# Down projections with one 512-column and one 256-column matmul per weight block

## The chip, the cores and the metric

The kernel runs on one core of a Trainium2 chip. The metric is device time in microseconds: the median of three runs, 1199.04 us before (1196.93 to 1201.48).

## The reference, cut to what matters

One layer of a hybrid decoder trunk on a sequence of 256 tokens with a model width of 2048, in float32: adaLN, a combined input projection, attention heads beside Mamba-2 heads, an output projection, and then a gated MLP with a causal depthwise convolution of width 3 over 5632 hidden channels. The change concerns the MLP's last product:

```python
def conv_ffn(h, w_up, conv_w, conv_b, w_down):
    u = causal_dwconv(h @ w_up, conv_w, conv_b)
    g, val = jnp.split(u, 2, axis=-1)
    return (jax.nn.silu(g) * val) @ w_down
...
x = x + gate_f * conv_ffn(h, w_up[l], conv_ffn_w[l], conv_ffn_b[l], w_down[l])
return rms_norm(x, final_norm_g)
```

## The kernel before, in words

All activations lie transposed: channels on the 128 partitions, the 256 tokens along the free axis. A float32 product is made from three matmuls in the format fp32r: weights w and activations a are each split into a high part (the value cast to fp32r) and a low part (the value less its high part), and the kernel adds w_hi·a_hi + w_hi·a_lo + w_lo·a_hi. `mm3` (lines 276 to 279) issues these three for one block of 128x128 weights; each is 256 columns wide and has a weight load of its own in the trace. An activation tile has 512 columns, the high part in the first 256 and the low part in the next 256.

Weights come in units. For a down projection a unit is 11 blocks (128 x 1408). SyncE's queue loads it, ScalarE casts it to the high part (line 258), VectorE subtracts to get the low part (line 259), in two parts of 8 and 3 blocks. High and low parts have four buffers each, so two units are ready or in use at a time, and the cast of a part waits until the part four back has been read by TensorE.

The MLP's 44 hidden tiles are done in two halves of 22. In each half the up projections fill 22 tiles `gts` of gated activations, and then a loop over the 16 column blocks i of the output (lines 803 to 822) multiplies them by the down weights: two units of 11 blocks, q = 0 and 1, added into one accumulator of 256 columns in PSUM, which has three accumulator buffers (`acc_tile`). There are 2 x 16 x 22 = 704 such blocks.

In half 0 two column blocks share a bank: block i even uses columns 0 to 255, i odd columns 256 to 511, and after the odd one ScalarE copies all 512 to `d0` (line 814). In half 1 each column block has a bank of its own; VectorE adds gate times `d0` to the residual stream x, then gate times the accumulator (`resid_add`, line 753). ScalarE squares x for the last norm (line 589), VectorE sums the squares, and ScalarE multiplies x by the norm's gain. Behind the sixteenth, three matmuls by ones sum over the partitions (lines 604 to 606), ScalarE takes the root, VectorE the reciprocal, and four products scale x and send it out.

The framework's scheduler sets each engine's order of instructions by a simulated timeline; an engine then works through its own queue in that order, with semaphore waits between engines.

The other products use the same helpers with other shapes: the value projections (line 348) stream 352 or 336 columns of weights, and the state space stage has a few matmuls of 512 columns in the same format (lines 557 and 558).

Of the kernel before, what the change touches and what calls it, by code (L numbers as in the profile page):

```python
# [18 lines left out]
T = 256  # L19
# [75 lines left out]
def hymba_layer(ctx, tc, xT, c_row, cT, w_ada, vecs, consts, relb, onehot, w_vdt, w_in, w_out, w_up1, w_up, w_dn, outT):  # L95
    nc = tc.nc
    dve, act, pool, pe = nc.vector, nc.scalar, nc.gpsimd, nc.tensor
# [30 lines left out]
    def acc_tile(name):  # L128
        return psp.tile([P, 512], F32, tag="acc", name=name, bufs=NACC)
# [63 lines left out]
    def V(name, i, n=1):  # L193
        return vec[:, CV[name] + i:CV[name] + i + n]
# [45 lines left out]
    def ada_some(n, last=24):  # L240
        for _ in range(n):
            g, i = ada_next[0]
            if g < last:
                ada_unit(g, i)
                ada_next[0] = [g, i + 1] if i < 3 else [g + 1, 0]
# [19 lines left out]
    def weight_unit(src, n, name, hw=1024):  # L265
        ws = get_unit(src, n, name)
        parts = [hi_lo_part(ws, o, min(hw, n - o), name) for o in range(0, n, hw)]

        def block(i):
            wh, wl = parts[i * P // hw]  # L270
            j = i * P % hw
            return wh[:, j:j + P], wl[:, j:j + P]

        return parts, block

    def mm3(o, whs, wls, a, first, last):
        pe.matmul(o, whs, a[:, 0:T], start=first, stop=False)  # L277
        pe.matmul(o, whs, a[:, T:2 * T], start=False, stop=False)  # L278
        pe.matmul(o, wls, a[:, 0:T], start=False, stop=last)  # L279

    def gemm_pair(acc, unit, b0, acts, npair=2):
        blk = unit[1]
        n = len(acts)
        for w in range(npair):
            o = acc[:, w * T:(w + 1) * T]
            for i, a in enumerate(acts):
                mm3(o, *blk(b0 + w * n + i), a, i == 0, i == n - 1)

    def gemm_part(o, unit, acts, first, last):
        blk = unit[1]  # L290
        n = len(acts)
        for i, a in enumerate(acts):
            mm3(o, *blk(i), a, first and i == 0, last and i == n - 1)


    def rstd_of(ps, n, name):
# [6 lines left out]
    def sqrt_ready(dep):  # L303
        act.activation(scr, dep, AF.Sqrt, bias=eps_t, scale=0.0)
# [120 lines left out]
    st = {}  # L425
# [158 lines left out]
    def sq_acc(i, name):  # L584
        if i == 0:
            act.activation(sqx, x[:, i, :], AF.Square)
        else:
            sq = tmp(f"sq_{name}", tag="psq", bufs=2)
            act.activation(sq, x[:, i, :], AF.Square)
            if i < 14:  # L590
                dve.tensor_add(sqx, sqx, sq)
            else:
                late_sq.append(sq)
# [100 lines left out]
    for i in range(6):  # L694
        pe.matmul(ss1[:, 0:T], ones, (sqs[:, 1, i * T:i * T + T] if i < 4 else sqs[:, 0, (i - 4) * T:(i - 3) * T]),
                  start=i == 0, stop=i == 5)
# [45 lines left out]
    def gate_up(j, us):  # L742
        g, v = (conv_ff(us[s], s * 44 + j, f"{j}_{s}") for s in range(2))
        act.activation(g, g, AF.Silu)
        dve.tensor_mul(v, g, v)
        gt = gp.tile([P, 512], F32R, tag="g", name=f"g{j}")
        hilo(gt, v)
        return gt

    d0 = fp.tile([P, KT, T], F32, name="d0")  # L750

    def resid_add(i, o, gate):
        dve.scalar_tensor_tensor(x[:, i, :], o, gate, x[:, i, :], op0=ALU.mult, op1=ALU.add)
# [15 lines left out]
    for j in range(NHALF):  # L769
        if j < NLEAD:  # L770
            acc = lead[j]
        else:
            u = weight_unit(w_up1[j], 2048, f"u1_{j}")
            acc = acc_tile(f"u1a{j}")
# [7 lines left out]
    for half in range(2):  # L782
        gts = []
        for jj in range(NHALF):
            j = half * NHALF + jj
            if half == 0:
                w = weight_unit(w_up1[NHALF + j], 2048, f"u2_{j}")
                acc = acc_tile(f"u2a{j}")
                gemm_pair(acc, w, 0, hk[8:])
                dve.tensor_add(parts[j], parts[j], acc)  # L790
                us = [parts[j][:, s * T:(s + 1) * T] for s in range(2)]
            else:
                acc = acc_tile(f"ua{j}")
                us = [acc[:, s * T:(s + 1) * T] for s in range(2)]
                for s in range(2):
                    gemm_part(us[s], weight_unit(w_up[2 * jj + s], 2048, f"u{j}_{s}"), hk, True, True)
            gts.append(gate_up(j, us))
            if half == 1:
                ada_some(1)
        if half == 1:  # L800
            ada_some(100)
            dve.tensor_add(par[:, 80:96], mod[:, 80:96], V("b_ada", 80, 16))
        for i in range(KT):
            if half == 0 and i % 2:
                o = acc[:, T:2 * T]
            else:
                acc = acc_tile(f"da{half}_{i}")
                o = acc[:, 0:T]
            for q in range(2):
                w = weight_unit(w_dn[half, i, q], 11 * P, f"d{half}_{i}_{q}")  # L810
                gemm_part(o, w, gts[11 * q:11 * q + 11], q == 0, q == 1)
            if half == 0:
                if i % 2:
                    act.copy(d0[:, i - 1:i + 1, :].rearrange("p a t -> p (a t)"), acc)
            else:
                gate = par[:, 80 + i:81 + i]
                resid_add(i, d0[:, i, :], gate)
                resid_add(i, o, gate)
                sq_acc(i, f"d{i}")
                act.activation(x[:, i, :], x[:, i, :], AF.Copy, scale=V("g_fin", i))  # L820
                if i == 0:
                    sqrt_ready(sqx[:, 0:1])
# [3 lines left out]
    for a, b in ((0, 2), (2, 6), (6, 11), (11, 16)):  # L826
        o = x[:, a:b, :]
# [89 lines left out]
```

## Time and profile before

| | |
|---|---|
| median of three runs | 1199.04 us |
| the profiled execution, its own time | 1196.57 us |
| its span, first to last instruction | 1194.8 us |
| matmuls on TensorE, busy | 1167.5 us, 9760 records |
| VectorE busy, ScalarE busy | 915.0 us, 636.9 us |
| mean granted clock | 0.988 |

Busy time of TensorE counts overlapping records once, and the ends of its records are modelled; the pace of a stream of matmuls is read from their starts. The first half's down projections run from about 703 to 824 us, the second half's from about 1068 to 1181.5.

### The profile page before, as it was taken

How to read it: one execution, taken by the hardware profiler on the slowest of the kernel's cores; microseconds unless marked ns; L12 is line 12 of the kernel's file. 1: busy time of each engine (PE TensorE's matmuls, PEld its weight loads, DVE VectorE, ACT ScalarE, POOL GpSimd, SP SyncE). 2: the span in 40 equal slices, each digit the busy share in tenths (PEclk: the TensorE clock that was granted, in tenths of full speed). 3: DMA queues.
4: the chain of work that ended last, by engine and by line, in shares of the span. 5: the costliest groups of instructions: out<-in, count | busy, mean ns of one | idle time of the engine just before them, and what ended most of it. 6: DMA issues, size and time to landing. Idle time of an engine off the chain costs nothing.

```text
span 1194.8 us, 23406 instructions
## 1 busy us (share of the span) xinstructions
PE 1167.5 (98%) x9760; PEld 1113.3 (93%) x9760; DVE 915.0 (77%) x1371; ACT 636.9 (53%) x959; POOL 0.9 (0%) x7
## 2 busy tenths in 40 slices
PE   6999999999999999999999999999999999999996
PEld 3899989988878898999999999999999999999995
DVE  6889979987988798786599984446888889656554
ACT  4544434457786544446567654444555555555552
POOL 0000000000000000000000000000000000000000
PEclk8899999999999999999999999999999999999998
DMA  9989988776765996997565545558878776545552
GB/s 359 409 338 337 327 335 304 276 268 246 287 242 214 365 383 237 343 357 245 183 204 186 201 146 194 195 194 276 295 299 301 284 282 227 196 150 196 194 194 96
DMA packets 47444, 309.60 MB, mean 259 GB/s; under 512 B 5568, under 2 KB 6761, under 8 KB 16105
## 3 DMA queue, kind: packets, MB, share of 16 engines
q1 hardware_dynamic: 46170, 307.04, 70.6%
q8 instruction: 76, 1.25, 0.4%
q10 hardware_dynamic: 1168, 1.06, 0.4%
q14 instruction: 30, 0.25, 0.1%
HBM read 305.98 MB, written 2.11 MB: 258 GB/s over the span
## 4 chain that ended last, share of the span: by engine, by line
PE 96%; DVE 1%; DMA 1%; ACT 1%; SPq 0%; issue 0%; DVEq 0%; ACTq 0%
PE ua L278 7%; PE ua L279 7%; PE da L279 7%; PE da L278 7%; PE da L277 7%; PE ua L277 7%; PE wa L277 6%; PE wa L279 6%; PE wa L278 6%; PE va L348 4%; PE u1a L278 3%; PE u1a L279 3%; PE u1a L277 3%; PE u2a L277 3%; PE u2a L279 3%; PE u2a L278 3%
## 5 line engine op out<-in xcount | busy, mean ns | idle before, releaser
L258 ACT CAST h_u<-s_u 128x1024 fp32r<-128x1024 f32 x176 | 183.6, 1050 | 188.3 <-PE ua L278 95.2
L259 DVE TENSOR_TENSOR l_u<-s_u,h_u 128x1024 fp32r<-128x1024 f32 x176 | 213.4, 1223 | 66.6 <-ACT h_u L258 64.6
L277 PE MATMUL ua<-h,h_u 128*128 128x256 f32 x704 | 194.3, 276 | 0.0
L278 PE MATMUL ua<-h,h_u 128*128 128x256 f32 x704 | 194.3, 276 | 0.0
L279 PE MATMUL ua<-h,l_u 128*128 128x256 f32 x704 | 194.3, 276 | 0.0
L279 PE MATMUL da<-g,l_d 128*128 128x256 f32 x704 | 194.3, 276 | 0.0
L278 PE MATMUL da<-g,h_d 128*128 128x256 f32 x704 | 194.3, 276 | 0.0
L277 PE MATMUL da<-g,h_d 128*128 128x256 f32 x704 | 194.1, 276 | 0.0
L259 DVE TENSOR_TENSOR l_d<-s_d,h_d 128x1024 fp32r<-128x1024 f32 (+1 forms) x128 | 108.8, 888 | 83.6 <-ACT h_d L258 83.6
L277 PE MATMUL wa<-hT,h_w 128*128 128x256 f32 x576 | 162.1, 282 | 0.8 <-ACT h_w L258 0.8
L279 PE MATMUL wa<-hT,l_w 128*128 128x256 f32 x576 | 159.8, 279 | 0.0
L278 PE MATMUL wa<-hT,h_w 128*128 128x256 f32 x576 | 159.7, 278 | 0.0
L258 ACT CAST h_d<-s_d 128x1024 fp32r<-128x1024 f32 (+1 forms) x128 | 98.2, 782 | 115.0 <-PE da L278 104.3
L210 DVE SCALAR_TENSOR_TENSOR ada<-ada,cb 128x2048 f32<-128x2048 f32 x60 | 137.2, 2288 | 11.5 <-DMA ada<-w_ada 11.2
L279 PEld LDWEIGHTS da<-g,l_d 128*128 128x128 f32 x704 | 132.2, 188 | 0.0
L277 PEld LDWEIGHTS ua<-h,h_u 128*128 128x128 f32 x704 | 132.2, 188 | 0.0
L278 PEld LDWEIGHTS ua<-h,h_u 128*128 128x128 f32 x704 | 132.2, 188 | 0.0
L279 PEld LDWEIGHTS ua<-h,l_u 128*128 128x128 f32 x704 | 132.2, 188 | 0.0
L278 PEld LDWEIGHTS da<-g,h_d 128*128 128x128 f32 x704 | 132.2, 188 | 0.0
L277 PEld LDWEIGHTS da<-g,h_d 128*128 128x128 f32 x704 | 132.1, 188 | 0.0
L258 ACT CAST h_w<-s_w 128x1024 fp32r<-128x1024 f32 x72 | 73.7, 1048 | 88.3 <-PE wa L278 42.7
L277 PEld LDWEIGHTS wa<-hT,h_w 128*128 128x128 f32 x576 | 108.4, 188 | 11.3 <-ACT h_w L258 3.6
(236 smaller groups left out, 2689.4 us busy)
## 6 DMA issues: line engine op xcount, KB each, us to landing
ada<-w_ada SPq DMA_DIRECT2D x96, 1024.0 KB, 6.1
s_u<-w_up SPq DMA_DIRECT2D x88, 1024.0 KB, 5.0
s_d<-w_dn SPq DMA_DIRECT2D x64, 704.0 KB, 4.1
s_w<-w_in SPq DMA_DIRECT2D x36, 1024.0 KB, 7.1
s_o<-w_out SPq DMA_DIRECT2D x16, 1024.0 KB, 8.3
s_v<-w_vdt SPq DMA_DIRECT2D x8, 1040.0 KB, 6.6
x<-xT SPq DMA_DIRECT2D x4, 512.0 KB, 4.8
outT<-x SPq DMA_DIRECT2D x2, 640.0 KB, 3.0
```

Of the source, the lines that this page charges most:

```text
L210: dve.scalar_tensor_tensor(ws[:, :D], ws[:, :D], 1.0, cb, op0=ALU.mult, op1=ALU.mult, accum_out=mod[:, j:j + 1])
L258: act.copy(wh[:, :m], ws[:, o:o + m])
L259: dve.tensor_sub(wl[:, :m], ws[:, o:o + m], wh[:, :m].bitcast(F32))
L277: pe.matmul(o, whs, a[:, 0:T], start=first, stop=False)
L278: pe.matmul(o, whs, a[:, T:2 * T], start=False, stop=False)
L279: pe.matmul(o, wls, a[:, 0:T], start=False, stop=last)
L348: pe.matmul(va[tt][i][:, :n], lo if st == 2 else hi, (wl if st == 1 else wh)[:, s], start=f and st == 0, stop=l and st == 2)
```

## The change

A new helper `gemm_full` takes the place of `gemm_part` in the down projections. It multiplies the high part of a weight block by all 512 columns of an activation tile at once, into all 512 columns of the accumulator's bank, so that w_hi·a_hi stands in the first 256 columns and w_hi·a_lo in the other 256; the low part of the weights is multiplied by the first 256 columns as before. In the last block the order of the two is turned round. Each column block has a bank of its own in both halves, and the two halves of the bank are added when it is read out: in half 0 ScalarE copies the first and VectorE adds the second to `d0`; in half 1 VectorE adds both to x, with the gate.

```diff
+    def gemm_full(acc, unit, acts, first, last):
+        blk = unit[1]
+        n = len(acts)
+        for i, a in enumerate(acts):
+            whs, wls = blk(i)
+            st, sp = first and i == 0, last and i == n - 1
+            if sp:
+                pe.matmul(acc[:, 0:T], wls, a[:, 0:T], start=False, stop=False)
+                pe.matmul(acc, whs, a, start=st, stop=True)
+            else:
+                pe.matmul(acc, whs, a, start=st, stop=False)
+                pe.matmul(acc[:, 0:T], wls, a[:, 0:T], start=False, stop=False)
...
         for i in range(KT):
-            if half == 0 and i % 2:
-                o = acc[:, T:2 * T]
-            else:
-                acc = acc_tile(f"da{half}_{i}")
-                o = acc[:, 0:T]
+            acc = acc_tile(f"da{half}_{i}")
             for q in range(2):
                 w = weight_unit(w_dn[half, i, q], 11 * P, f"d{half}_{i}_{q}")
-                gemm_part(o, w, gts[11 * q:11 * q + 11], q == 0, q == 1)
+                gemm_full(acc, w, gts[11 * q:11 * q + 11], q == 0, q == 1)
             if half == 0:
-                if i % 2:
-                    act.copy(d0[:, i - 1:i + 1, :].rearrange("p a t -> p (a t)"), acc)
+                act.copy(d0[:, i, :], acc[:, 0:T])
+                dve.tensor_add(d0[:, i, :], d0[:, i, :], acc[:, T:2 * T])
             else:
                 gate = par[:, 80 + i:81 + i]
                 resid_add(i, d0[:, i, :], gate)
-                resid_add(i, o, gate)
+                resid_add(i, acc[:, T:2 * T], gate)
+                resid_add(i, acc[:, 0:T], gate)
```

## Rows read from the trace of the kernel before

**Rows 1.** The page: busy us and share by engine, slices, chain that ended last.

```profile
PE 1167.5 (98%) x9760; PEld 1113.3 (93%) x9760; DVE 915.0 (77%) x1371; ACT 636.9 (53%) x959; POOL 0.9 (0%) x7
...
PE   6999999999999999999999999999999999999996
PEld 3899989988878898999999999999999999999995
...
PE 96%; DVE 1%; DMA 1%; ACT 1%; SPq 0%; issue 0%; DVEq 0%; ACTq 0%
```

**Rows 2.** The tile da: duration ns min/median/max, first and last start us, forms.

```profile
L277 PE MATMUL da<-g,h_d x704: 276/276/276, 702.9 to 1181.3; 128*128 128x256 f32 x176
...
L279 PE MATMUL da<-g,l_d x704: 276/276/277, 703.2 to 1181.5; 128*128 128x256 f32 x176
L753 DVE SCALAR_TENSOR_TENSOR x<-da,par,x x16: 483/484/485, 1071.1 to 1181.9; 128x256 f32<-128x256 f32 x16
L814 ACT COPY d<-da x8: 580/581/582, 718.4 to 823.7; 128x512 f32<-128x512 f32 x8
```

**Rows 3.** Timeline of TensorE, 740 to 745 (start us, busy us); 47 rows.

```profile
739.76 0.28 PE L278 MATMUL da<-g,h_d 128*128 128x256 f32 x1
739.88 0.28 PE L279 MATMUL da<-g,l_d 128*128 128x256 f32 x1
...
744.98 0.28 PE L279 MATMUL da<-g,l_d 128*128 128x256 f32 x1
```

**Rows 4.** Windows: us, busy and count by engine, granted clock, DMA share, GB/s.

```profile
1086.00:1181.00 95.00, 95.00 (x841) 95.00 (x840) 50.07 (x74) 48.10 (x73) 0.00 (x0) 1.00 0.51 168
```

**Rows 5.** Timeline of TensorE, state space stage: 512 columns and what follows.

```profile
333.85 0.39 PE L558 MATMUL sg<-am,tri_r 128*128 128x512 f32 x1
334.08 0.28 PE L559 MATMUL sg<-am,ones_r 128*128 128x256 f32 x1
...
345.64 0.39 PE L558 MATMUL sg<-am,tri_r 128*128 128x512 f32 x1
345.86 0.28 PE L559 MATMUL sg<-am,ones_r 128*128 128x256 f32 x1
...
346.58 0.28 PE L277 MATMUL oa<-cat,h_o 128*128 128x256 f32 x1
...
374.50 0.40 PE L558 MATMUL sg<-am,tri_r 128*128 128x512 f32 x1
374.75 0.28 PE L559 MATMUL sg<-am,ones_r 128*128 128x256 f32 x1
```

**Rows 6.** Chain in order of time (start us, us): the value projections.

```profile
170.43 11.40 PE va L348 x72
```

**Rows 7.** Timeline of TensorE beside the value projections; nine rows.

```profile
228.33 0.28 PE L278 MATMUL wa<-hT,h_w 128*128 128x256 f32 x1
...
229.27 0.33 PE L348 MATMUL va<-l_v,hT 128*128 128x352 f32 x1
```

**Rows 8.** Lines by form, 900 to the end: busy us, mean ns, idle before.

```profile
L259 DVE TENSOR_TENSOR l_d<-s_d,h_d 128x1024 fp32r<-128x1024 f32 x32 | 39.1, 1221 | 23.0 <-ACT h_d L258 23.0
L258 ACT CAST h_d<-s_d 128x1024 fp32r<-128x1024 f32 x32 | 33.6, 1049 | 47.6 <-PE da L278 45.5 <-issue 1.2 <-PE ua L278 0.8
...
L737 ACT ACTIVATE fo<-ua,vec 128x256 f32<-128x256 f32 x32 | 17.9, 559 | 1.4 <-DVE fo L739 1.4
```

**Rows 9.** Waits, 1071 to 1181: us in total, times, longest us.

```profile
ACT h_d L258 <- PE da L278: 45.2, 28, 2.2
```

**Rows 10.** Timeline of ScalarE and VectorE, 1173.2 to 1176.

```profile
1173.24 1.53 ACT L258 CAST h_d<-s_d 128x1024 fp32r<-128x1024 f32 x2 [2.21 <-PE da L278]
...
1174.37 0.48 DVE L753 SCALAR_TENSOR_TENSOR x<-da,par,x 128x256 f32<-128x256 f32 x1 [2.10 <-PE da L279]
1174.77 1.69 DVE L259 TENSOR_TENSOR l_d<-s_d,h_d 128x1024 fp32r<-128x1024 f32 x2
```

**Rows 11.** Chain in order of time, from 1181 to the end.

```profile
1181.70 0.13 PE da L279
1181.83 0.03 issue
1181.86 0.49 DVE x L753
1182.35 0.02 issue
1182.37 0.42 ACT sq_d L589
1182.80 0.04 issue
1182.84 0.71 PE ssx L606 x2
```

## The prediction

> **What bounds the kernel now.** I read the page from the top: the engine totals, the slices and the chain of waits. The reader is to see in [rows 1] that TensorE's matmuls fill 98% of the span, that both middle rows of the slices hold nines from the third slice to the last but one, and that TensorE makes 96% of the chain that ended last. Next I read the down projections' tile: 2112 matmuls of 256 columns, 704 from each of three lines, all at one duration [rows 2]. Their ends are modelled, so I take the pace from their starts in the timeline: 47 rows from 739.76 to 744.98 are 46 steps in 5.22 us, or 113.5 ns a matmul [rows 3]. A long stretch of the second half's down projections shows TensorE and its weight loads busy for all of 95.00 us, at a granted clock of 1.00 [rows 4]. At the upper of the two clock levels, 2.4 GHz, 256 columns are 106.7 ns, so each matmul carries 6.8 ns beyond its columns. A block is three of them now: 340.4 ns. All 704 blocks make 239.6 us, and this is the only time that the change can move, apart from the end of the kernel.
>
> **The change part by part.**
>
> *The matmuls.* Each block loses one 256-column matmul and its weight load, and another becomes 512 columns wide. The columns stay at 768. So nothing of the 320 ns that the columns take at 2.4 GHz goes away; what can change is the 20.4 ns beside them. The sum is 704 blocks times the change of one block, and all depends on two paces: that of a 512-column matmul of this number format with a new weight load before and after it, and that of a 256-column one standing alone between two such.
>
> The first has near rows: the state space stage issues 512-column matmuls of the same format, and the one of line 558 is followed at once by a 256-column one. The steps are 334.08 − 333.85 = 0.23, 345.86 − 345.64 = 0.22 and 374.75 − 374.50 = 0.25 us (the rows round to 0.01) [rows 5]. The line runs eight times, and over the eight I read a mean of 231.5 ns. That is 18 ns beyond its 213.3 ns of columns, against 6.8 for a narrow one: the excess grows with the width. The value projections say the same: 72 matmuls of 352 and 336 columns (mean 346.7) in 11.40 us are 158.3 ns each, 13.9 beyond the 144.4 of their columns [rows 6]. Bounds for 512 columns: from below 213.3 + 6.8 = 220.1 ns (the excess is a fixed part of a matmul, as the steady pace would have it), from above 0.24 to 0.25 us [rows 5]. I take 0.230.
>
> The narrow one: 113.5 ns in the steady stretch [rows 3], but from 345.86 to 346.58, right behind the wide ones, six steps take 0.72 us, or 120 ns [rows 5], and beside the value projections eight take 229.27 − 228.33 = 0.94 us, or 117.5 ns [rows 7]. Both stretches run the same line 277 to 279 helpers as the down projections. So there are two paces, and the quick one is seen where only 256-column matmuls follow one another for long. Below, the bound is 113.5; above, 120. Which of the two the narrow one takes between wide ones no row shows; I take 116.
>
> A block is then 230 + 116 = 346 ns, against 340.4: 5.6 ns more, and 704 times that is +3.9 us. The ends: 220.1 + 113.5 = 333.6 gives −4.8 us; 245 + 120 = 365 would give +17.3, but that takes the slowest single pair for all; with the mean of the pairs, 231.5 + 120 = 351.5, it is +7.8 us.
>
> A rule from the Trainium skill, page "TensorE: Matmul & The Clock Gate", section "Back-to-back issue gap", speaks of a warm gap of N/2.4 + 2.5 ns. By it a block would go from 327.5 to 325.0 ns, −1.8 us in all. The trace does not agree: 113.5 against the page's 109.2 at 256 columns, and 231.5 against 215.8 at 512, and the misfit grows with the width, which speaks against the change.
>
> *Evictions of the first half.* Eight copies of 128x512 at 581 ns [rows 2] become sixteen copies of 256 columns and sixteen adds of 256 columns on VectorE. ScalarE's nearest row with 256 columns out of PSUM is line 737 at 559 ns, VectorE's is line 753 at 484 [rows 8, 2]: at most 8.9 us on ScalarE in place of 4.6, and 7.7 more on VectorE, over 120 us. The add waits for the copy, and what is queued behind it on VectorE is the next subtraction of line 259, on which TensorE waits in turn. The cover: ScalarE's cast of the next-but-one weight unit sits idle until TensorE frees its buffer (45.2 us over 28 times in the second half's stretch) [rows 9]. At that point TensorE still has the last three blocks of this unit and the eleven of the next one, 14 x 0.340 = 4.76 us, while cast and subtraction need 1.05 + 1.22 = 2.27 [rows 8]. The eviction falls 1.02 us into these 4.76; copy and add (1.04 us, behind the second cast that ends 1.53 us in) end at about 2.6 us, and a subtraction held until then is done at 3.8. So 0.9 us are left and I cost it at nothing. If that cover is gone, each of the sixteen costs what it overruns, up to about 0.5 us, which is the third rival.
>
> *Evictions of the second half.* One more multiply-add on VectorE a column block, 484 ns each. In the present trace line 753 holds the subtraction until 1174.85 after a cast that began at 1173.24 [rows 10]; 0.48 later it still ends at about 1176.6, and TensorE needs it at 1173.24 + 4.76 = 1178.0. Nothing, fifteen times of sixteen.
>
> *The end.* The sixteenth is on the path: the last matmul, then line 753 for 0.49 us, the square, the sums, the root [rows 11]. Both halves of the last accumulator come with the last matmul, so two such adds stand in a row: +0.5 us. The first half's value can be added before, as now.
>
> *PSUM.* The first half uses sixteen banks in turn where eight served; there are three buffers, and a bank is filled for 22 blocks, 7.5 us, so a late eviction of 2 us blocks nobody. Weight transfers keep their sizes and order.
>
> Sum: +3.9 + 0.5 = +4.4 us. The profiled execution took 1196.57 (span 1194.8 and 1.8 around it), so it would be 1201.0 there. The median of the runs lies 2.5 us higher, at 1199.04; on that footing the forecast is 1203.4.
>
> **The rivals.**
>
> *A: the saved matmul is a gain.* For it speaks that the steady stretch is the stage in question, and that its excess may be a fixed part (220.1 + 113.5, −4.8 us), or may come from the weight load: weight loads are busy 93% of the span [rows 1], one each 113.5 ns, and if these set the pace, dropping one in three leaves 213.3 to 216 ns of stream plus 113.5, 11 ns less, −7.7 us. With the end's +0.5: −4.3 to −7.2, or 1194.7 to 1191.8. Against it: in [rows 5, 6] a wide matmul hides its successor's load easily and still carries 14 to 18 ns.
>
> *B: the pace goes by columns.* 512 columns cost twice 113.5 and the narrow one stays: no change but the end, 1199.5. For it: 231.5 lies 4 ns above 227, and those pairs stand beside interruptions.
>
> *C: slower by a new wait.* In the first half the add waits for ScalarE, which may put the copy behind casts that themselves wait for TensorE; then VectorE holds the subtraction for the following unit and TensorE runs dry at that unit's first narrow matmul. It decides when copy and add end more than 3.5 us after the buffer was freed (4.76 less 1.22). At 0.5 us for each of sixteen this is +8 on top of the +4.4: 1211. Against it: 2.6 us in the working above, and idle time on both engines.
>
> **How the numbers follow.** About 0.5% (6 us) is what a measurement of this kernel tells from no change. The forecast has 55%: its own range is 1200 to 1207, and beyond 1205 it counts as slower (17 of the 55, with 231.5 + 120 and a little more). A has 27%, of which 10 lie below 1193. B has 12%, C 6%. So faster 10, within 17 + 12 + 38 = 67, slower 17 + 6 = 23. The range from 1193 to 1208.5 leaves out the quick end of A and C with the slowest pairs.
>
> **What would show it.** In the changed trace: starts of the down projections' wide matmuls to the next narrow one at 225 to 235 ns (220 or less is A, 227 with 113.5 is B), narrow to wide at 113 to 120. Copies of 256 columns 16 times and two line-753 kinds out of PSUM, with no idle time of TensorE ahead of a narrow matmul (C would show it there, released by VectorE). The chain at the end with two adds, 1.0 us in place of 0.49. The prediction is wrong in its core if the block's pace falls under 338 ns.

## The result, and the profile after

The changed kernel takes 1205.33 us (median of 6 runs, 1204.95 to 1209.15) against 1197.67 before (6 runs): a ratio of 1.0068, with a 95% interval from 1.0053 to 1.0084. So it is slower, by 6 to 10 us. The profiled execution took 1204.95 us, its span is 1203.0.

First the page of the kernel after, the engine totals, to set beside [rows 1]:

```profile
PE 1174.3 (98%) x9056; PEld 1089.3 (91%) x9056; DVE 927.6 (77%) x1403; ACT 634.9 (53%) x967; POOL 0.9 (0%) x7
```

There are 704 matmuls and 704 weight loads fewer, weight loads are busy 24 us less, and matmuls 7 us more. Next the down projections by window, the first half and the second (us, then busy time and count of matmuls, weight loads, VectorE, ScalarE and GpSimd, granted clock, DMA share, GB/s):

```profile
701.00:828.00 127.00, 127.00 (x733) 111.28 (x732) 66.00 (x91) 57.68 (x86) 0.00 (x0) 1.00 0.57 192
...
1070.00:1189.00 119.00, 119.00 (x677) 103.88 (x677) 67.75 (x104) 57.49 (x90) 0.00 (x0) 1.00 0.49 164
```

TensorE is busy for all of both windows at a granted clock of 1.00, as in [rows 4]: the clock did not fall, and no wait of TensorE shows. It is the pace that changed. The tile of the down projections, first in the trace of before over the first half (duration min/median/max in ns, first and last start in us):

```profile
L277 PE MATMUL da<-g,h_d x352: 276/276/276, 702.9 to 822.3; 128*128 128x256 f32 x176
...
L279 PE MATMUL da<-g,l_d x352: 276/276/276, 703.2 to 822.5; 128*128 128x256 f32 x176
```

The same in the trace of after, over the first half and then over the second:

```profile
L305 PE MATMUL da<-g,h_d x336: 388/397/400, 701.7 to 825.0; 128*128 128x512 f32 x168
...
L303 PE MATMUL da<-g,h_d x16: 394/394/401, 711.7 to 825.4; 128*128 128x512 f32 x16
...
L305 PE MATMUL da<-g,h_d x336: 388/397/400, 1065.0 to 1188.7; 128*128 128x512 f32 x168
...
L303 PE MATMUL da<-g,h_d x16: 393/394/397, 1075.0 to 1189.2; 128*128 128x512 f32 x16
```

From the first start to the last a half takes 825.4 − 701.7 = 123.7 and 1189.2 − 1065.0 = 124.2 us. Before, it was 822.5 − 702.9 = 119.6 us, 1055 steps of 113.3 ns. That is +4.1 and +4.6, or 8.7 us. The timeline shows where it sits; it answers to [rows 3]:

```profile
740.45 0.39 PE L305 MATMUL da<-g,h_d 128*128 128x512 f32 x1
740.67 0.28 PE L306 MATMUL da<-g,l_d 128*128 128x256 f32 x1
740.79 0.40 PE L305 MATMUL da<-g,h_d 128*128 128x512 f32 x1
741.02 0.28 PE L306 MATMUL da<-g,l_d 128*128 128x256 f32 x1
741.14 0.40 PE L305 MATMUL da<-g,h_d 128*128 128x512 f32 x1
741.38 0.28 PE L306 MATMUL da<-g,l_d 128*128 128x256 f32 x1
741.50 0.39 PE L305 MATMUL da<-g,h_d 128*128 128x512 f32 x1
```

Wide to narrow is 0.22 to 0.24, narrow to wide 0.12. Over both halves a wide one takes a mean of 233.0 ns to the next start (225 to 238) and a narrow one 119.3 (113 to 124, but for one step of 305). A block is 352.3 ns where three times 113.3 made 340.0: 12.3 ns more, times 704 = 8.7 us. The narrow matmul, which the change does not touch, lost 6.0 of the 12.3 ns; the wide one takes 6.3 more than the two that it stands for.

The step of 305 ns stands here, and it is why the second half lost 0.4 us more than the first:

```profile
1181.47 0.59 PE L617 MATMUL ssx<-sqx,ones 128*128 128x256 f32 x2
1181.71 0.47 PE L306 MATMUL da<-g,l_d 128*128 128x256 f32 x1
1182.01 0.39 PE L305 MATMUL da<-g,h_d 128*128 128x512 f32 x1
```

A first sum for the last norm (line 617; line 604 before), which stood behind the last down projection in the trace of before, now lies among them: 1182.01 − 1181.47 = 0.54 us, of which a narrow matmul needs 0.12. So some 8.3 of the 8.7 us are pace and 0.4 is this. (By starts the pace makes 8.3, by blocks 8.7, because the starts leave out the last matmul of each half, 0.1 us longer now that it is wide, and take in the turned blocks, which are a little quicker.)

The other part is the end, which answers to [rows 11] (chain in order of time):

```profile
1189.33 0.24 PE da L303
...
1189.60 0.50 DVE x L766
...
1190.12 0.50 DVE x L766
...
1190.63 0.42 ACT sq_d L602
```

Two adds where one stood: from the end of the last matmul to the square 1.06 us, 0.52 more than before. In all 8.7 + 0.5 = 9.2, while the spans differ by 8.2: in this execution the down projections began 1.2 us earlier (701.7 against 702.9 in [rows 2]), in stages that the change leaves alone. Over all traces of this study that start lies between 701.7 and 705.3, so this share is taken for scatter.

### The profile page after: what moved, and what is told of

It is laid out like the page before. It is cut to its first block, busy times and chain, and to the rows that moved or that the text cites. A ratio compares the mean times of both kernels' runs of the same rounds, so it can differ in the third digit from the quotient of the medians.

```text
span 1203.0 us, 21994 instructions
## 1 busy us (share of the span) xinstructions
PE 1174.3 (98%) x9056; PEld 1089.3 (91%) x9056; DVE 927.6 (77%) x1403; ACT 634.9 (53%) x967; POOL 0.9 (0%) x7
## 3 DMA queue, kind: packets, MB, share of 16 engines
q10 hardware_dynamic: 1168, 1.06, 0.4%
## 4 chain that ended last, share of the span: by engine, by line
PE 95%; DVE 2%; DMA 1%; ACT 1%; SPq 0%; issue 0%; DVEq 0%; ACTq 0%
PE da L305 13%; PE da L306 7%; PE ua L278 7%; PE ua L279 7%; PE ua L277 7%; PE wa L277 6%; PE wa L279 6%; PE wa L278 5%; PE va L361 4%; PE u2a L278 3%; PE u2a L279 3%; PE u2a L277 3%; PE u1a L278 3%; PE u1a L279 3%; PE u1a L277 3%; PE adp L217 3%
## 5 line engine op out<-in xcount | busy, mean ns | idle before, releaser
L305 PE MATMUL da<-g,h_d 128*128 128x512 f32 x672 | 238.1, 395 | 0.0
L306 PE MATMUL da<-g,l_d 128*128 128x256 f32 x672 | 189.5, 282 | 0.0
L259 DVE TENSOR_TENSOR l_d<-s_d,h_d 128x1024 fp32r<-128x1024 f32 (+1 forms) x128 | 111.2, 887 | 75.9 <-ACT h_d L258 75.9
L305 PEld LDWEIGHTS da<-g,h_d 128*128 128x128 f32 x672 | 126.3, 188 | 28.7
L306 PEld LDWEIGHTS da<-g,l_d 128*128 128x128 f32 x672 | 126.4, 188 | 1.3
L277 PEld LDWEIGHTS wa<-hT,h_w 128*128 128x128 f32 x576 | 108.5, 188 | 11.2 <-issue 4.2
L279 PEld LDWEIGHTS wa<-hT,l_w 128*128 128x128 f32 x576 | 107.8, 188 | 2.6 <-issue 0.8
L278 PEld LDWEIGHTS wa<-hT,h_w 128*128 128x128 f32 x576 | 108.2, 188 | 0.1
```

Source lines behind the costliest of these rows:

```text
L259: dve.tensor_sub(wl[:, :m], ws[:, o:o + m], wh[:, :m].bitcast(F32))
L305: pe.matmul(acc, whs, a, start=st, stop=False)
L306: pe.matmul(acc[:, 0:T], wls, a[:, 0:T], start=False, stop=False)
```

## The experiments

**Three narrow matmuls, with the new evictions.**

```diff
-                pe.matmul(acc, whs, a, start=st, stop=False)
-                pe.matmul(acc[:, 0:T], wls, a[:, 0:T], start=False, stop=False)
+            pe.matmul(acc[:, 0:256], whs, a[:, 0:256], start=st, stop=False)
+            pe.matmul(acb[:, 0:256], whs, a[:, 256:512], start=st, stop=sp)
+            pe.matmul(acc[:, 0:T], wls, a[:, 0:T], start=False, stop=sp)
```

> Three 256-column matmuls a block again, but with the changed kernel's evictions: the high part times the second 256 columns goes to a PSUM bank of its own and is added when it is read out. Theory W (the time went into the pace of the matmuls, and only a stream of nothing but 256-column matmuls runs at 113.3 ns): all steps at 113.3 ns, about 1198.2 us, that is the kernel before plus 0.5 us for the second add at the end. Rival E (the evictions or the order of the engines' work cost it): stays at 1204 to 1206. Rival K (two accumulators open at once break the quick pace): steps at 117 to 118, 1206 to 1208.

Measured: 1197.73 us (10 runs) against 1197.18 before, ratio 0.9996 (0.9977 to 1.0015). The timeline, the first two and the last of 13 rows:

```profile
739.78 0.28 PE L301 MATMUL da<-g,h_d 128*128 128x256 f32 x1
739.89 0.28 PE L302 MATMUL db<-g,h_d 128*128 128x256 f32 x1
...
741.14 0.28 PE L301 MATMUL da<-g,h_d 128*128 128x256 f32 x1
```

Twelve steps in 1.36 us are 113.3 ns, with a change of accumulator at two steps of every three. The evictions, the extra adds and the order of the engines' work cost at most what the interval leaves, 1.8 us. Rivals E and K fall; the loss is the matmuls' pace. (Here the norm's first sum stands behind the last down projection again.)

**Wide and narrow ones grouped by unit.**

```diff
+            for i, a in enumerate(acts):
+                pe.matmul(acc, blk(i)[0], a, start=first and i == 0, stop=False)
+            for i, a in enumerate(acts):
+                pe.matmul(acc[:, 0:T], blk(i)[1], a[:, 0:T], start=False, stop=False)
```

> Same matmuls as in the changed kernel, but in each unit the eleven 512-column ones come in a row and then the eleven 256-column ones (the other way round in the second unit). Theory W1 (every 512-column matmul costs about 232 ns whatever stands beside it; a 256-column one is at 113.3 ns among its like, after some that settle): a block of 345 to 349 ns, 1201 to 1205 us. Theory W2 (the cost is the change of width, wide ones among their like run at 220 or less): a block of 333 to 336, 1193 to 1196 us. Theory W3 (the narrow ones don't get back to the quick pace within eleven): 232 + 118 = 350, 1205 us, as the changed kernel.

Measured: 1203.43 us (10 runs), ratio 1.0042 (1.0021 to 1.0062). The timeline merges each group of eleven into a row:

```profile
740.95 2.69 PE L302 MATMUL da<-g,h_d 128*128 128x512 f32 x11
743.49 2.71 PE L305 MATMUL da<-g,h_d 128*128 128x512 f32 x11
746.03 1.46 PE L307 MATMUL da<-g,l_d 128*128 128x256 f32 x11
747.33 1.46 PE L300 MATMUL da<-g,l_d 128*128 128x256 f32 x11
...
753.70 1.41 PE L307 MATMUL da<-g,l_d 128*128 128x256 f32 x11
754.95 1.41 PE L300 MATMUL da<-g,l_d 128*128 128x256 f32 x11
```

Eleven wide ones take 2.54 us, 230.9 ns each, among their like: W2 falls, a wide matmul is slow by itself and not by the change of width. Next to narrow ones they take 233.0, so only 2 ns are from the change of width. Of the narrow groups one takes 747.33 − 746.03 = 1.30 us (118 ns each) and another 754.95 − 753.70 = 1.25 (114): some find the quick pace again and some don't, so W1 and W3 each hold for a part, and their mean is 116 ns. It is not random: from the third column block of either half on, both groups of one column block run at 113 to 114 ns and both of the next at 118, in strict turns to the end. What sets the turns no run shows. By the medians the kernel lies between the one before and the changed one, though its interval overlaps that of the changed one (1.0053 to 1.0084).

**Three matmuls a block, of 272, 240 and 256 columns.**

```diff
+            pe.matmul(acc[:, 0:272], whs, a[:, 0:272], start=st, stop=False)
+            pe.matmul(acb[:, 0:240], whs, a[:, 272:512], start=st, stop=sp)
+            pe.matmul(acc[:, 0:T], wls, a[:, 0:T], start=False, stop=sp)
```

> As the kernel with three narrow matmuls, but with 272 and 240 columns in place of 256 and 256 for the two with the high part, so that three matmuls and 768 columns a block stay (the output columns are then put together wrongly; only the time is read). Theory W (the quick pace belongs to an unbroken series of 256 columns alone): a block of 350 to 360 ns, 1205 to 1213 us. Rival P (the excess goes in proportion to the width beyond what a weight load covers, so widths close to 256 cost what 256 costs): a block of 339 to 343 ns, 1198 to 1200 us.

Measured: 1209.7 us (4 runs), ratio 1.0101 (1.0064 to 1.0139). The timeline:

```profile
739.78 0.29 PE L301 MATMUL da<-g,h_d 128*128 128x272 f32 x1
739.91 0.28 PE L302 MATMUL db<-g,h_d 128*128 128x240 f32 x1
740.02 0.28 PE L303 MATMUL da<-g,l_d 128*128 128x256 f32 x1
...
740.85 0.29 PE L301 MATMUL da<-g,h_d 128*128 128x272 f32 x1
```

Three blocks in 1.07 us are 357 ns each, and over both halves the mean is 356: 16 more than three times 256 columns, though the columns and the count are the same. The matmul of 272 columns takes 125.2 ns, that of 240 takes 111.7, and that of 256, whose width stays, 119.3 in place of 113.3: 10 of the 16 ns are from the uneven pair and 6 from its neighbour. Theory W holds, rival P falls. By the pace, sixteen columns moved from one matmul to its neighbour cost more than the change under study (16 ns a block against 12.3); the kernels' ratios overlap in their intervals.

**A row of widths.**

```diff
+            if width and not st and not sp:
+                pe.matmul(acc[:, 0:width], whs, a[:, 0:width], start=False, stop=False)
+                pe.matmul(acc[:, 0:width], wls, a[:, 0:width], start=False, stop=False)
```

> The down projections as a measuring row: each column block i has both its matmuls (high and low part) at one width, from 128 to 512 columns by i, with 256 in between as a control, except the first and the last weight block of i (the output leaves out or doubles parts; only the starts of the matmuls are read). Theory W: 256 alone settles at 113.3 ns, and every other width above it runs 4 to 5 per cent over its columns at 2.4 GHz plus some ns (264 at about 121, 288 at 132, 320 at 146, 352 at 160, 384 at 175, 448 at 203, 512 at 232). Rival F (a fixed 6.7 ns a matmul when the series is uniform): 264 at 116.7, 288 at 126.7, 352 at 153.3, 384 at 166.7, 512 at 220. Rival L (weight loads pace the narrow ones): every width from 128 to 256 at 110 to 113.3, and above 256 a jump.

One execution; the granted clock is 1.00 in both stages. The timeline, the first and the last row of three widths (40 rows each for 512 and 264 columns, 39 for 256):

```profile
702.48 0.40 PE L305 MATMUL da<-g,h_d 128*128 128x512 f32 x1
711.47 0.39 PE L306 MATMUL da<-g,l_d 128*128 128x512 f32 x1
...
712.64 0.28 PE L305 MATMUL da<-g,h_d 128*128 128x256 f32 x1
716.95 0.28 PE L308 MATMUL da<-g,l_d 128*128 128x256 f32 x1
...
717.64 0.28 PE L305 MATMUL da<-g,h_d 128*128 128x264 f32 x1
722.35 0.28 PE L306 MATMUL da<-g,l_d 128*128 128x264 f32 x1
```

Steps are one fewer than rows: 8.99 / 39 = 230.5 ns for 512, 4.31 / 38 = 113.4 for 256, 4.71 / 39 = 120.8 for 264. The means for most of the widths, from the unrounded starts, beside what the columns take at 2.4 GHz:

| columns | 160 | 208 | 240 | 248 | 256 | 264 | 288 | 320 | 352 | 384 | 448 | 512 |
|---|---|---|---|---|---|---|---|---|---|---|---|---|
| ns a matmul | 110.6 | 111.2 | 111.9 | 113.3 | 113.3 to 118 | 120.7 | 132.4 | 146.3 | 160.0 | 173.8 | 201.1 | 230.6 |
| columns alone | 66.7 | 86.7 | 100.0 | 103.3 | 106.7 | 110.0 | 120.0 | 133.3 | 146.7 | 160.0 | 186.7 | 213.3 |

(192 and 224 columns are left out: steps of 0.2 to 0.7 us lie in them. Of the other widths, 128 columns take 110.3 ns, 252 take 114.9 and 260 take 120.3.) Below 256 columns the pace hardly depends on the width, as rival L had it: no width here has a mean under 110 ns. That the weight load sets this floor is likely but not shown, since no run pairs a narrow stream with a shorter load. Above, the pace grows by (230.6 − 120.7) / 248 = 0.443 ns a column where 2.4 GHz makes 0.417. Rival F, the fixed part, falls everywhere above 256. Theory W's numbers hold to 2 ns above 256, but one sentence of it fails: 256 columns did not settle at 113.3 each time. Of the nine control blocks the one shown kept 113.3 throughout; six had means of 115.0 to 117.9, and two more had long steps in them. Where one of these six or two found the quick pace, it did so only after 14 or more steps at about 118, and then kept it to its end or to the next long step.

**Other engines silent; activations zero.**

```diff
+        if half == 0:
+            kept = [weight_unit(w_dn[0, 0, q], 11 * P, f"d0_0_{q}") for q in range(2)]
+        else:
+            z = gp.tile([P, 512], F32R, tag="g", name="zero")
+            act.activation(z, gts[0].bitcast(F32), AF.Copy, scale=0.0)
+            gts = [z] * NHALF
...
+                w = kept[q] if half == 0 else weight_unit(w_dn[half, i, q], 11 * P, f"d{half}_{i}_{q}")
```

> Same pairs of 512 and 256 columns. In the first half the weights of one column block are loaded and cast once and used for all sixteen, so that DMA, ScalarE and VectorE have next to nothing to do there; in the second half everything runs as in the changed kernel, but the activations are all zero (outputs are left wrong; only the starts of the matmuls are read). Theory I (the excess belongs to TensorE's own stream in this format): 233 and 119 ns in both halves. Rival S (the streams of the other engines and of the DMAs hold up the reads): the first half falls to 220 or less and 113, the second stays at 233. Rival D (it goes with the operands' values): the second half falls to 220 or less, the first stays.

The windows of a stretch of the first half, and the timelines of both halves:

```profile
740.00:820.00 80.00, 80.00 (x456) 69.88 (x455) 4.21 (x10) 3.73 (x10) 0.00 (x0) 1.00 0.00 1
```

```profile
740.15 0.40 PE L305 MATMUL da<-g,h_d 128*128 128x512 f32 x1
740.39 0.28 PE L306 MATMUL da<-g,l_d 128*128 128x256 f32 x1
...
740.85 0.40 PE L305 MATMUL da<-g,h_d 128*128 128x512 f32 x1
...
1119.62 0.40 PE L305 MATMUL da<-zero,h_d 128*128 128x512 f32 x1
1119.85 0.28 PE L306 MATMUL da<-zero,l_d 128*128 128x256 f32 x1
...
1120.68 0.40 PE L305 MATMUL da<-zero,h_d 128*128 128x512 f32 x1
```

In the first half the DMA share is 0.00, VectorE and ScalarE work 4 of 80 us, and the steps keep a mean of 233.0 and 119.3 ns. With zeros three pairs take 1.06 us, 353 ns each (median steps 233 and 118). Theory I holds: neither the other engines' traffic nor the activations' values make the excess (the weights kept their values). (The execution's 1216.3 us hold a wait of TensorE for the zeros, 5.2 us, at the start of the second half, and 5 us behind it at a granted clock of 0.50, the lower level; they say nothing on the pace.)

**Half the weight load; bfloat16.**

```diff
+                pe.matmul(acc[0:64, :], whs[:, 0:64], a, start=False, stop=False)
+                pe.matmul(acc[0:64, 0:T], wls[:, 0:64], a[:, 0:T], start=False, stop=False)
...
+                pe.matmul(acc, b16[:, 512:640], b16[:, 0:512], start=False, stop=False)
+                pe.matmul(acc[:, 0:T], b16[:, 640:768], b16[:, 0:T], start=False, stop=False)
```

> Same pairs of 512 and 256 columns, except in the first and the last weight block of each column block. In the first half the weight loads are 64 columns wide in place of 128 (half of the outputs is left out), in the second half all operands are bfloat16 tiles made once (the products are replaced by others). Theory I (the stream of this format takes some 4 to 8 per cent beyond its columns, whatever the load): 230 to 233 and 117 to 119 ns in the first half; in the second half 216 and 109. Rival H (the handover from one weight load to the next makes the excess): the first half falls by 5 ns or more a matmul. Rival G (the excess is that of any matmul of this width): the second half stays at 230.

The timelines, three pairs of each half:

```profile
739.91 0.39 PE L308 MATMUL da<-g,h_d 128*64 128x512 f32 x1
740.14 0.28 PE L309 MATMUL da<-g,l_d 128*64 128x256 f32 x1
...
740.94 0.39 PE L308 MATMUL da<-g,h_d 128*64 128x512 f32 x1
...
1100.87 0.38 PE L311 MATMUL da<-b 128*128 128x512 bf16 x1
1101.09 0.27 PE L312 MATMUL da<-b 128*128 128x256 bf16 x1
...
1101.85 0.38 PE L311 MATMUL da<-b 128*128 128x512 bf16 x1
```

With half the load, three pairs take 1.03 us, 343 ns each; the means are 229.0 and 115.3. That is 4 ns less for either matmul than in the changed kernel: less than rival H asked for, a little more than theory I allowed. The load's length has a small share, and 229.0 still lies 15.7 above the columns. In bfloat16 three pairs take 0.98 us, 327 ns each, at a granted clock of 1.00, and the median steps are 216 and 109 ns: the excess is gone, and rival G falls. So it belongs to the format, but this run changes two things at once, as the rows of the weight loads show:

```profile
L309 PEld LDWEIGHTS da<-g,l_d x320: 133/134/138, 704.3 to 824.8; 128*64 128x64 f32 x160
...
L311 PEld LDWEIGHTS <-b x320: 96/98/151, 1074.3 to 1189.6; 128*128 128x128 bf16 x160
```

The load's row is 188 ns in the changed kernel, 134 with half the columns and 98 in bfloat16. The 54 ns from the first to the second gave 4 ns a matmul; at that rate the 36 from the second to the third would give 2.7 (an estimate), of the 13 by which the wide matmul falls from 229.0 and the 6 by which the narrow one falls from 115.3. That the rest is the stream itself is argued from this, not shown.

## Why the prediction was right, and what in it was too small

**The time** lies in the range (1193 to 1208.5), and the sign of the forecast is right: 1203.4 was said, 1205.3 measured. But the forecast was a step of +4.4 us, and the measured one is 7.7 between the medians, 8.1 by the ratio. That 1203.4 came so near is in part luck: it was added to 1199.04, the median of three runs, where six give 1197.67, and on that footing it would have been 1202.1. Most of the chance, 67 in 100, lay on no difference of 0.5%, and the interval (from 0.53%) lies beyond that: it came out in the part to which 23 were given.

**The term that was mis-sized** is the block: +5.6 ns predicted (230 + 116), +12.3 measured (233.0 + 119.3), times 704. The wide matmul was read from eight pairs of another stage at 231.5, written down as 230, and came at 233.0; that source was good. The narrow one was set at 116, midway between the steady pace and the 117.5 to 120 of [rows 5, 7], though no row showed any of the quick pace beside other widths. It came at 119.3, inside those rows. The rows right behind the wide ones [rows 5] were the nearest, and the midpoint with the steady stretch had no row behind it: 3.3 ns of the 6.7 missing are from it, 3.0 from the wide one, and 0.4 from reading the block of before as 340.4 for 340.0. One reading there was loose: of the six steps behind the wide ones four belong to lines 559 to 562 and only two to the helper of lines 277 to 279, and right after them that trace has the quick pace (line 277 at 346.58, the next start at 346.69). So what the rows showed is a slow pace next to other widths, and the changed stage never leaves that neighbourhood.

**Evictions at nothing:** right. With three narrow matmuls and the same evictions the kernel is at 0.9996 of before. ScalarE's copies took 0.37 us and VectorE's adds 0.41, less than the bounds; no row of TensorE shows a wait for either. (The working takes line 753 to hold the subtraction until 1174.85; [rows 10] have it begin at 1174.77. Nothing hangs on the difference.)

**The end at +0.5 us:** right, two adds of 0.50 in a row. What the sum had at nothing without a word is the order of TensorE's own work: the norm's first sum moved into the stage and cost 0.4 us there.

**Rival A,** that the saved matmul is a gain, fell in both its forms. The fixed part of 6.8 ns a matmul does not exist above 256 columns, as the row of widths shows. There is a floor (about 111 ns), as a pace set by weight loads would have it, but 256 columns lie 2 ns above that floor already, and a wide matmul does not reach its 216 ns even when the load is halved. **Rival B,** pace by columns with the narrow one as before, was 6 ns too good for the wide matmul and 6 for the narrow one. **Rival C,** a new wait, did not show.

**The rule from the Trainium skill** ("TensorE: Matmul & The Clock Gate", section "Back-to-back issue gap"), which the page gives for a matmul by itself, was weighed rightly: its 215.8 and 109.2 ns are what the bfloat16 pairs show (216 and 109), and the fp32r pairs do not follow it (233.0 and 119.3).

What the runs leave open is why an unbroken series of 256 columns holds 113.3 ns, what lets it find that pace or miss it, and why the fp32r stream takes 0.443 ns more for each column above 256.

## What to carry to other kernels

Two matmuls made into one wide one save nothing by their number: read the pace of the wide form from the starts of a stage that already uses it, and compare it with the pace in place, not with the columns alone. In fp32r an unbroken series of 256 columns is the best form measured here, at 113.3 / 256 = 0.443 ns a column: below, the floor of some 111 ns is paid for fewer columns; 512 columns take 0.450. But 256 columns that miss the quick pace take 118 / 256 = 0.461, and three of them (354 ns) cost as much as the changed block (352.3). What the kernel before had over the changed one is the quick pace, and one odd width in a series costs its 256-column neighbours that pace. Where an edit changes a matmul's neighbours, price the neighbours from rows beside such a form, not from the steady stretch.

## What the runs showed of the hardware that was not expected

- Moving 16 columns from one matmul to the next (272, 240, 256 in place of 3 x 256) costs 16 ns a block of 340 and 12 us in the kernel; 6 of the 16 ns fall on the matmul whose width stays.
- The same pairs take 352.3 ns in fp32r and 325 (216 + 109, by the medians) in bfloat16, at the same granted clock of 1.00; silent neighbours and zero activations change nothing (352.3 and, by the medians, 351).
- A matmul with a 128-column weight load takes about 111 ns whether it streams 160 or 240 columns (110.6 and 111.9).
- The quick pace of 256 columns comes and goes: groups of eleven run at 114 or at 118 ns in the same stage, in strict turns by column block, without a wait of TensorE between them.
